# Encoder trunk with three token mixers: both passes over a block traced with a scheduling priority of 4000

## The chip, the cores and the metric

The kernel runs on one core of one Trainium2 chip. The metric is the device time of one execution in microseconds (us). TensorE (PE) does the matmuls, VectorE (DVE) and ScalarE (ACT) the element-wise work, GpSimd (POOL) a little of it, and SyncE (SP) issues most of the transfers.

## The reference, cut to what matters

Two sequences (256 and 2048 rows of 1024) go through one encoder layer. Each layer has a projection whose columns feed three mixers, each of which scans the sequence forward and backward in chunks; then an output projection, a gated feed-forward block and norms.

```python
h = _rmsnorm(x, prm['norm_mix'][l])
p = h @ prm['w_in'][l]
pg, pr, ps = _split(p, [GLA_COLS, RWKV_COLS, SSD_COLS])
o_gla  = _gla_mixer(pg, ...)     # forward scan + strict backward scan
o_rwkv = _rwkv7_mixer(pr, ...)   # the same, with a 64x64 state per head
o_ssd  = _ssd_mixer(ps, ...)     # the same, after a convolution over 5 rows
mix = jnp.concatenate([o_gla, o_rwkv, o_ssd], axis=-1)
x = x + mix @ prm['w_out'][l]
h = _rmsnorm(x, prm['norm_ffn'][l])
x = x + (jax.nn.silu(h @ prm['ffn_gate'][l]) * (h @ prm['ffn_up'][l])) @ prm['ffn_down'][l]
return _rmsnorm(x, prm['final_norm'])
```

## The kernel before, in words

The 2304 rows are cut into nine blocks of 256 (block 0 is the prompt, 1 to 8 the sample) and, for the wide matmuls, into groups of up to 512 rows (the sample's begin at rows 256, 768, 1280 and 1792).

There are two kinds of work. **Panels** are the wide matmuls: `in_chan` and `in_tok` (input projection), `out_proj`, and the steps of `ffn`. A panel loads 256 columns of a weight (`wr`), splits them into a high and a low part (`wh` on ACT, `wl` on DVE), and runs three matmuls for each 128 rows of the contraction, in fp32r, with the full 128x128 array, into PSUM tiles `d` and `g`. The normed and transposed input of a group sits in the tile pair `hT`, of which there is one: the next group's four transposes and copies (`norm_T`, L371) wait until the last panel of a group has read it.

**Passes** are the mixers. `pass_a(b)` does the forward scans of block b and stores what the backward scan needs; `pass_b(b)` does the backward scans and leaves the result in the tile pair `mix`, which `out_proj(b)` reads. A pass is a long chain of small fp32 matmuls (PSUM tiles `s`, `c`, `a` and, in `pass_a`, `g`) with DVE and ACT instructions between them. Many of these matmuls use a part of the array: `prod` (in `rwkv_local`) multiplies 32x32 pieces, 32 matmuls to a product, into two `s` tiles, `rwkv_chain` works on 64x64 pieces into `c`.

All instructions are traced once, in the order in which the Python runs; a scheduler then orders them on each engine: of the instructions that are ready it takes the one with the lowest number first, which is its place in the trace. `high_priority(offset=n)` traces a stretch with n taken off that number. Before the change this is used for norms alone (offset 3000, in `normed` and in `ffn`). `run` sets the trace order: panels of a group, then `pass_a` of the blocks that are complete, then the next group; later `second(...)` yields after each `pass_b`, and two steps of `ffn` follow each yield. `first` and `second` are the two closures that call the passes.

Every matmul goes through `mm`, so the profile gives all of them line 118; they are told apart by their tiles.

Of the kernel before, what the change touches and what calls it, by code (L numbers as in the profile page):

```python
# [70 lines left out]
class Encoder:  # L71
# [1066 lines left out]
    def run(self):  # L1138
        self.setup()
        prompt = [(t, min(GS, self.Lp - t)) for t in range(0, self.Lp, GS)]  # L1140
        sample = [(t, min(GS, self.NT - t)) for t in range(self.Lp, self.NT, GS)]
        done, st, sb, self.rs2, self.ready = 0, None, None, {}, {}

        def first(end):

            nonlocal done, st
            while done < self.NB:
                lo, hi = self.seq(done)
                need = (done + 1) * TB
                if need > end or (need == end and need != hi):  # L1150
                    break
                if done * TB == lo:
                    st = self.states()
                self.pass_a(done, st)
                done += 1

        def second(t0, n):

            nonlocal sb
            mix = None  # L1160
            for b in range((t0 + n) // TB - 1, t0 // TB - 1, -1):
                if (b + 1) * TB == self.seq(b)[1]:
                    sb = self.states()
                if mix is not None:
                    self.out_proj(b + 1, mix)
                mix = self.pass_b(b, sb)
                self.free = False
                yield
            self.out_proj(t0 // TB, mix)

        def run(*steps):

            steps = list(steps)
            while steps:
                for s, k in list(steps):
                    for _ in range(k):
                        if next(s, steps) is steps:
                            steps.remove((s, k))
                            break

        def emit(steps, k=None):
            while (k is None or k > 0) and next(steps, steps) is not steps:
                k = k and k - 1

        order = sample[::-1]
        self.last = order[0][0]
        for t0, n in prompt:
            emit(self.in_proj(t0, n))
            if t0 == 0:
                self.setup_mixers()  # L1190
            first(t0 + n)
        ahead = [second(*g) for g in reversed(prompt)]
        for k, (t0, n) in enumerate(sample):
            dense = self.in_proj(t0, n, 2 if k or len(sample) == 1 else 0)
            if k == 1 or k == len(sample) - 1:
                for s in ahead:
                    emit(s, 1)
                    emit(dense, 5)
                    emit(s)
                ahead = []  # L1200
                first(t0)
            if k > 0 or len(sample) == 1:
                emit(dense, 11)
                first(t0 + n)
            emit(dense)
        if len(sample) > 1:
            emit(self.in_proj(*sample[0], 1))
        early = [self.ffn(*g, inside=g[1] <= TB) for g in prompt]
        for f in early:
            emit(f, 2)  # L1210
        rest = [self.ffn(*g, after) for g, after in zip(order, order[1:] + [None])]
        for k, f in enumerate(early + rest):
            steps = [(second(*order[k]), 1)] if k < len(order) else []
            run(*steps, (f, 2))
# [30 lines left out]
```

## Time and profile before

| | |
|---|---|
| median of 3 runs | 3809.86 us (3805.5 to 3811.69) |
| the profiled execution | 3807.3 us, span 3805.4 us |
| PE busy | 3574.5 us, 94% |
| DVE busy | 2417.1 us, 64% |
| ACT busy | 1464.8 us, 38% |
| POOL busy | 589.9 us, 16% |
| mean granted TensorE clock | 0.963 of 2.4 GHz |

The span is the time between the first and the last instruction; the profiled execution's own time is 1.9 us more. Matmuls are pipelined, so PE's busy time is an upper bound of its work. The granted clock of a stretch is a mean over two levels, 1.2 and 2.4 GHz: 0.77 means that the clock was at 1.2 GHz for 46% of that stretch.

### The profile page before, as it was taken

The numbers are of one execution on the slowest core, as the hardware profiler recorded it, in microseconds if no ns is written. First come the engines' busy times: TensorE is split into PE (matmuls) and PEld (weight loads), VectorE is DVE, ScalarE is ACT, GpSimd is POOL, SyncE is SP. The second block draws the span as 40 slices with busy tenths as digits, with TensorE's granted clock in tenths as the row PEclk, the third lists the DMA queues.
The fourth block names the chain that finished last, engine by engine and source line by source line (L and its number), as shares of the span: only waits on it lengthen the run. The fifth ranks groups of instructions, "written<-read, shape, count | busy, mean of one in ns | idle before, by whom it ended". The sixth has DMA issues, their size and how long they took to land.

```text
span 3805.4 us, 84415 instructions
## 1 busy us (share of the span) xinstructions
PE 3574.5 (94%) x34142; PEld 3002.8 (79%) x34142; DVE 2417.1 (64%) x5533; ACT 1464.8 (38%) x3282; POOL 589.9 (16%) x618
## 2 busy tenths in 40 slices
PE   6899889899989989998989999999999999999998
PEld 6677667677767767887978888888888888888887
DVE  5943496785883798876757564665655565545444
ACT  4623253543553455443433232323233232332222
POOL 3422123242332333211000000000000000000000
PEclk9999899899989989998989999999999999999999
DMA  6544243334334433554644343434343442434332
GB/s 180 169 143 126 84 144 114 118 106 134 120 97 126 128 115 121 167 170 142 192 134 136 113 140 116 141 114 131 117 139 115 131 137 86 148 100 139 94 95 95
DMA packets 430230, 486.87 MB, mean 128 GB/s; under 512 B 49344, under 2 KB 389584, under 8 KB 428688
## 3 DMA queue, kind: packets, MB, share of 16 engines
q1 hardware_dynamic: 390720, 422.40, 36.4%
q10 hardware_dynamic: 38112, 55.40, 4.1%
q8 instruction: 269, 4.41, 0.5%
q0 software_dynamic: 1008, 3.67, 0.3%
q14 instruction: 121, 0.99, 0.1%
HBM read 395.18 MB, written 86.18 MB: 126 GB/s over the span
## 4 chain that ended last, share of the span: by engine, by line
PE 73%; DVE 15%; DMA 6%; ACT 3%; issue 3%; POOL 0%; ACTq 0%; SPq 0%; DVEq 0%; POOLq 0%
PE d L118 46%; PE g L118 15%; PE s L118 4%; PE a L118 3%; PE c L118 3%; DVE mix L104 3%; DVE wl L94 1%; DMA mix<-d_xb 1%; DMA x<-d_x 1%; DVE mix L94 1%; PE d L371 1%; DVE b4a L94 1%; DMA qg<-q_g 1%; DVE b9x L104 1%; ACT wh L111 1%
## 5 line engine op out<-in xcount | busy, mean ns | idle before, releaser
L118 PE MATMUL d<-hT,wh 128*128 128x512 f32 (+3 forms) x4384 | 1276.7, 376 | 19.3 <-DVE ev L115 10.0
L111 ACT ACTIVATE wh<-wr 128x512 fp32r<-128x512 f32 (+1 forms) x1084 | 624.8, 621 | 1146.0 <-PE d L118 638.0
L94 DVE TENSOR_TENSOR wl<-wr,wh 128x512 fp32r<-128x512 f32 x944 | 650.8, 717 | 475.2 <-ACT wh L111 471.2
L118 PEld LDWEIGHTS d<-hT,wh 128*128 128x128 f32 (+1 forms) x4384 | 791.2, 191 | 174.1 <-issue 13.3
L118 PE MATMUL d<-hT,wl 128*128 128x512 f32 (+3 forms) x2192 | 813.0, 374 | 8.5 <-DVE wl L94 8.4
L118 PEld LDWEIGHTS d<-hT,wl 128*128 128x128 f32 (+1 forms) x2192 | 417.2, 191 | 85.9 <-DVE wl L94 11.4
L94 POOL TENSOR_TENSOR wl<-wr,wh 128x512 fp32r<-128x512 f32 (+1 forms) x140 | 202.0, 1444 | 583.7 <-ACT wh L111 519.5
L118 PE MATMUL g<-hT,wh 128*128 128x512 f32 x896 | 282.3, 394 | 0.0
L118 PE MATMUL d<-wh,b 128*128 128x256 f32 x928 | 267.3, 289 | 3.3 <-DVE b4d L94 2.4
L118 PE MATMUL d<-wl,b 128*128 128x256 f32 x928 | 259.9, 281 | 0.0
L118 PE MATMUL d<-wh,b9x 128*128 128x256 f32 x928 | 258.6, 282 | 0.0
L118 PE MATMUL d<-wh,hT 128*128 128x256 f32 x1216 | 251.1, 298 | 3.2 <-DVE ev L115 2.4
L118 PEld LDWEIGHTS d<-wh,hT 128*128 128x128 f32 x1216 | 200.5, 197 | 14.6 <-issue 4.7
L118 PEld LDWEIGHTS g<-hT,wh 128*128 128x128 f32 x896 | 166.3, 188 | 34.4 <-issue 0.3
L118 PE MATMUL d<-wh,mix 128*128 128x256 f32 x832 | 173.6, 295 | 10.1 <-ACT mix L111 7.5
L118 PEld LDWEIGHTS d<-wh,b 128*128 128x128 f32 x928 | 174.8, 188 | 10.0 <-DVE b4d L94 3.0
L118 PE MATMUL d<-wl,hT 128*128 128x256 f32 x608 | 177.4, 294 | 3.6 <-DVE wl L94 3.6
L118 PEld LDWEIGHTS d<-wl,b 128*128 128x128 f32 x928 | 174.9, 189 | 0.9
L118 PE MATMUL g<-hT,wl 128*128 128x512 f32 x448 | 175.1, 391 | 0.0
L118 PEld LDWEIGHTS d<-wh,b9x 128*128 128x128 f32 x928 | 174.2, 189 | 0.7 <-issue 0.3
L118 PEld LDWEIGHTS d<-wh,mix 128*128 128x128 f32 x832 | 138.1, 196 | 13.7 <-ACT mix L111 8.4
L118 PE MATMUL g<-wh,b 128*128 128x256 f32 x480 | 140.0, 292 | 2.3 <-DVE b4a L94 2.0
(387 smaller groups left out, 6149.7 us busy)
## 6 DMA issues: line engine op xcount, KB each, us to landing
wr<-in_w_in SPq DMA_DIRECT2D x260, 256.0 KB, 3.1
wr<-in_ffn_gate SPq DMA_DIRECT2D x220, 256.0 KB, 2.8
wr<-in_ffn_up SPq DMA_DIRECT2D x220, 256.0 KB, 2.9
wr<-in_ffn_down SPq DMA_DIRECT2D x220, 256.0 KB, 2.9
wr<-in_w_out SPq DMA_DIRECT2D x144, 256.0 KB, 3.1
x<-in_x_sample SPq DMA_DIRECT2D x20, 512.0 KB, 3.9
x<-d_x SPq DMA_DIRECT2D x20, 512.0 KB, 3.8
q_s<-qs ACTq DMA_DIRECT2D x18, 520.0 KB, 3.4
```

What stands on the lines that cost most here:

```text
L94: (eng or self.nc.vector).tensor_tensor(out=out, in0=a, in1=b, op=op)
L104: (eng or self.nc.vector).scalar_tensor_tensor(out=out, in0=a, scalar=s, in1=b, op0=op0, op1=op1)
L111: self.nc.scalar.activation(out=out, in_=in_, func=AF.Copy)
L118: self.nc.tensor.matmul(out, lhsT=lhsT, rhs=rhs, start=start, stop=stop, tile_position=tp, skip_group_check=lax)
L371: self.nc.tensor.transpose(ps[:, k * P:(k + 1) * P], h[:, (4 * q + k) * P:(4 * q + k + 1) * P], self.c["ident"])
```

## The change

Each pass is traced in a `high_priority(offset=4000)` block. No instruction is added, removed or altered; their order on the engines changes.

```diff
@@ -1151,7 +1151,8 @@
                     break
                 if done * TB == lo:
                     st = self.states()
-                self.pass_a(done, st)
+                with self.tc.high_priority(offset=4000):
+                    self.pass_a(done, st)
                 done += 1
 
         def second(t0, n):
@@ -1163,7 +1164,8 @@
                     sb = self.states()
                 if mix is not None:
                     self.out_proj(b + 1, mix)
-                mix = self.pass_b(b, sb)
+                with self.tc.high_priority(offset=4000):
+                    mix = self.pass_b(b, sb)
                 self.free = False
                 yield
             self.out_proj(t0 // TB, mix)
```

**First place, PE at the end of `pass_b` of block 0.** `s_4062`, `s_4068`, `a_4130` and `a_4167` belong to that pass, `c_5684`, `s_5182`, `s_5183`, `s_5196`, `s_5197` to `pass_a` of block 1, and `d_4812` is the first panel of `out_proj` of block 0, which reads the pass's result. PE's rows before the change:

```order
L118 MATMUL s_4062<-qy_3511,cf 128x256 x2
L118 MATMUL c_5684<-b9x_5157,gup 128x256 x2
L118 MATMUL s_4068<-cf,b2a_4066 128x2 x4
L118 MATMUL s_5182<-b9x_5157,wup 64x256 x4
L118 MATMUL s_5183<-b9x_5157,wup 64x256 x4
L118 MATMUL s_4068<-ident,b2a_4066 128x128 x4
L118 MATMUL s_5196<-b9x_5157,aup 64x256 x4
L118 MATMUL a_4130<-cf,b2a_4128 128x2 x4
L118 MATMUL a_4167<-sS_3500,scb_4160 128x256 x2
L118 MATMUL s_5197<-b9x_5157,aup 64x256 x4
L118 MATMUL a_4130<-ident,b2a_4128 128x128 x4
L118 MATMUL d_4812<-wh,mix_199_3502 128x256
```

After the change (`d_4423` is the first panel of the group of row 768):

```order
L118 MATMUL d_4423<-hT_4240,wh 128x512
L118 MATMUL d_4423<-hT_4241,wh 128x512
L118 MATMUL d_4423<-hT_4240,wl 128x512
L118 MATMUL a_4130<-cf,b2a_4128 128x2 x4
L118 MATMUL a_4167<-sS_3500,scb_4160 128x256 x2
L118 MATMUL s_5197<-b9x_5157,aup 64x256 x4
L118 MATMUL d_4423<-hT_4240,wh 128x512
L118 MATMUL d_4423<-hT_4241,wh 128x512
L118 MATMUL d_4423<-hT_4240,wl 128x512
```

Before, the five panels of that group stand ahead of the end of the pass, and between `s_4062` and `d_4812` no panel matmul stands. After it the end of the pass has moved ahead of most of them: between `s_4062` and the last matmul into `a_4130` stand 83 panel matmuls of 512 columns.

**Second place, PE in the first product of `pass_b` of block 4**, written to `s_28130` and `s_28131`; the rows into `g` and `d` are panels (before: of `out_proj` of block 5). Before:

```order
L118 MATMUL g_26491<-wl,mix_1921_24512 128x256
L118 MATMUL g_26491<-wh,mix_1922_24513 128x256
L118 MATMUL s_28130<-BK_28051,qg_28061 32x32 x3
L118 MATMUL s_28131<-BK_28051,qg_28061 32x32
L118 MATMUL d_26490<-wh,mix_1921_24512 128x256
L118 MATMUL g_26491<-wh,mix_1921_24512 128x256
L118 MATMUL s_28131<-BK_28051,qg_28061 32x32 x3
L118 MATMUL s_28130<-BK_28051,qg_28061 32x32
L118 MATMUL d_26490<-wl,mix_1921_24512 128x256
L118 MATMUL d_26490<-wh,mix_1922_24513 128x256
```

After, with panels of `ffn` around it:

```order
L118 MATMUL d_25644<-wh,b_2010_25250 128x256
L118 MATMUL d_25644<-wl,b_2010_25250 128x256
L118 MATMUL s_28130<-BK_28051,qg_28061 32x32 x4
L118 MATMUL s_28131<-BK_28051,qg_28061 32x32 x4
L118 MATMUL s_28130<-BK_28051,qg_28061 32x32 x4
L118 MATMUL s_28131<-BK_28051,qg_28061 32x32 x4
L118 MATMUL s_28130<-BK_28051,qg_28061 32x32 x4
L118 MATMUL s_28131<-BK_28051,qg_28061 32x32 x4
L118 MATMUL s_28130<-BK_28051,qg_28061 32x32 x4
L118 MATMUL s_28131<-BK_28051,qg_28061 32x32 x4
L118 MATMUL d_25644<-wh,b9x_25251 128x256
```

The same 32 matmuls stand in nine pieces before, strewn among panels, and in one piece after.

## Rows read from the trace of the kernel before

**Rows 1.** The page: span, busy time of each engine, chain by engine.

```profile
span 3805.4 us, 84415 instructions
...
PE 3574.5 (94%) x34142; PEld 3002.8 (79%) x34142; DVE 2417.1 (64%) x5533; ACT 1464.8 (38%) x3282; POOL 589.9 (16%) x618
...
PE 73%; DVE 15%; DMA 6%; ACT 3%; issue 3%; POOL 0%; ACTq 0%; SPq 0%; DVEq 0%; POOLq 0%
```

**Rows 2.** Busy time by stretch: stretch, length, engines (records), PEclk, DMA share, GB/s.

```profile
428.00:511.00 83.00, 64.00 (x518) 53.42 (x518) 64.04 (x166) 30.59 (x70) 11.95 (x13) 0.77 0.37 114
...
688.00:750.00 62.00, 47.57 (x845) 32.16 (x837) 54.45 (x126) 41.51 (x116) 22.43 (x26) 0.88 0.36 108
...
1049.00:1102.00 53.00, 41.42 (x422) 30.75 (x421) 52.28 (x133) 31.25 (x81) 16.00 (x19) 0.77 0.32 96
...
1367.00:1412.00 45.00, 33.29 (x318) 23.63 (x319) 41.30 (x101) 27.42 (x69) 17.08 (x18) 0.81 0.33 102
...
1719.00:1751.00 32.00, 23.66 (x240) 19.48 (x238) 18.08 (x56) 4.52 (x10) 4.68 (x6) 0.68 0.30 97
1751.00:1905.00 154.00, 150.77 (x1894) 140.06 (x1895) 116.35 (x308) 69.71 (x171) 11.77 (x14) 0.99 0.59 184
1905.00:1940.00 35.00, 25.17 (x531) 20.75 (x532) 21.41 (x63) 11.62 (x31) 0.79 (x2) 0.71 0.56 184
1940.00:3255.00 1315.00, 1298.91 (x11391) 1114.36 (x11391) 788.03 (x1860) 423.85 (x908) 76.34 (x85) 1.00 0.39 123
3255.00:3805.00 550.00, 531.02 (x3124) 470.09 (x3123) 271.10 (x574) 170.23 (x343) 1.14 (x2) 0.99 0.35 112
```

**Rows 3.** Timeline of PE, 428 to 475: rows with idle before them.

```profile
431.71 1.98 PE L118 MATMUL s<-qy,cf 128*128 128x256 f32 x4 [0.72 <-DVE qy L94]
...
453.61 2.08 PE L118 MATMUL a<-ident,b2a 128*128 128x128 f32 x8 [3.54 <-DVE b2a L104]
461.13 0.58 PE L118 MATMUL d<-wh,mix 128*128 128x256 f32 x1 [5.45 <-ACT mix L111]
469.26 0.99 PE L1054 MATMUL a<-ident,b2b 128*128 128x128 f32 x4 [2.87 <-DVE b2b L104]
```

**Rows 4.** Timeline of PE in a torn product, 2262.7 to 2265.3: start, us.

```profile
2262.73 0.28 PE L118 MATMUL g<-wh,mix 128*128 128x256 f32 x1
2262.85 0.28 PE L118 MATMUL g<-wl,mix 128*128 128x256 f32 x1
...
2264.02 0.28 PE L118 MATMUL g<-wh,mix 128*128 128x256 f32 x1
2264.23 0.26 PE L118 MATMUL s<-BK,qg 32*32 32x32 f32 x8
2264.43 0.38 PE L118 MATMUL d<-wh,mix 128*128 128x256 f32 x1
2264.65 0.28 PE L118 MATMUL g<-wh,mix 128*128 128x256 f32 x1
2264.86 0.26 PE L118 MATMUL s<-BK,qg 32*32 32x32 f32 x8
2265.05 0.39 PE L118 MATMUL d<-wl,mix 128*128 128x256 f32 x1
```

**Rows 5.** Timeline of PE where a product stands in one piece.

```profile
1004.76 0.76 PE L118 MATMUL s<-W,BK 32*32 32x32 f32 x64
1005.44 0.69 PE L118 MATMUL c<-UV,SC 128*64 128x64 f32 x16
```

**Rows 6.** Timeline of PE: an fp32 transpose on the full array between panel matmuls.

```profile
2198.70 0.39 PE L118 MATMUL d<-hT,wl 128*128 128x512 f32 x1
2198.93 0.39 PE L118 MATMUL d<-hT,wh 128*128 128x512 f32 x1
2199.16 1.05 PE L118 MATMUL s<-ident,b2a 128*128 128x128 f32 x8
```

**Rows 7.** The costliest groups: a panel's matmuls that read `wl`.

```profile
L118 PE MATMUL d<-hT,wl 128*128 128x512 f32 (+3 forms) x2192 | 813.0, 374 | 8.5 <-DVE wl L94 8.4
```

## The prediction

> **What bounds the kernel now.** I read the page first: PE is busy 94% of the span, and the chain that ended last is PE for 73% and DVE for 15% [rows 1]. So the end is set by PE's work and by the places where PE waits. The busy times by stretch say where those are. From 1940 to 3255 us, where `ffn` panels run beside `pass_b` of blocks 5 to 1, PE is busy 1298.9 of 1315 us at full clock; from 3255 on there are panels alone [rows 2]. There only less PE work helps. Before 1940 there are short stretches in which PE waits: 19.0 us of 83 are idle from 428 to 511, and in the three stretches in which `hT` is filled anew for the next group (from 688, 1049 and 1367) PE is busy 122.3 of 160 us while DVE is busy 148.0 of 160. In all four the granted clock is 0.77 to 0.88 [rows 2]: after the idling PE works part of the time at 1.2 GHz, so an idle microsecond there costs more than itself. The timeline says what the first stretch is: the end of `pass_b` of block 0, a chain with nothing beside it. PE waits 3.54 us for DVE's `b2a`, then 5.45 us before the first matmul of `out_proj`, for `mix` [rows 3]. From the matmul into `s` at 431.71 to the one into `a` at 453.61 that is 22 us without a panel.
>
> **What the change moves.** Panels and passes compete for PE, DVE, ACT and the queues. Before, a panel traced ahead of a pass goes first whenever it is ready, and the pass gets what is left over; now a pass goes first and the panels fill. The work is the same, so only the order can pay, and I looked in the two built orders for what changes at the places above. Durations are from the trace, counts from the orders.
>
> *The end of block 0's pass.* It now stands ahead of most of the group of row 768: 83 panel matmuls of 512 columns lie between the pass's `s_4062` and the last one into `a_4130`, where before there was none. Such matmuls follow each other after 0.23 us [rows 6], so that is 19 us of cover for a chain that took 22. What the stretch loses now: 19.0 us idle, and the clock. At 0.77 it ran at 1.2 GHz for 46% of 83 us, 38 us; if all of the idle time lay within those, 19 us of work took twice its time (9.5 us lost), and if none did, 38 (19 lost). So 28.5 to 38 us are lost, of which I take **25** as won, since 19 of 22 us are covered and `pass_a` of block 1 has waits of its own there. Bounds: nothing (the waits turn up again under that pass) and 38.
>
> *Torn products.* In the stretch from 1940 to 3255 the products of `rwkv_local` come in pieces, since panels went first: the first one of block 4's pass stands in nine pieces among panels, and after the change in one. What a piece costs is in the timeline. Panel matmuls of 256 columns start 0.12 us apart; where the next one is a 32x32 matmul it starts 0.21 us later, so 0.09 more. The four matmuls (eight records) then hold PE for 0.20 us before the panel goes on [rows 4]; as a part of a whole product, 64 records in 0.68 us [rows 5], eight take 0.085. So there is another 0.115, and a piece pays 0.2 us, **0.10 for each change** of the part of the array in use. It isn't fp32 that costs: an fp32 transpose on the full 128x128 starts 0.23 us after a panel matmul, as the next panel matmul does [rows 6]. So I counted in both orders where neighbouring matmuls use a different part of the array. Among the matmuls that ran from 1940 to 3255: 552 before, 328 after. From 1612 to 1940: 204 and 161. Before 1612: 720 and 696. In the first two stretches 267 fewer by 0.10 is **26.7 us**; the 24 earlier ones I put at nothing, since PE waits for DVE in much of that part. In the long stretch PE idles 16 of 1315 us, so little there can swallow the gain. Bounds: nothing, and 291 by 0.10, 29.
>
> The Trainium skill has two rules for this. "TensorE: Matmul & The Clock Gate" (Step-by-step: what each phase is for) says that the drain of one matmul overlaps the fill of the next, so that a stream is spaced by its columns alone; by that a torn product costs nothing, and the sum would lack this term. "TensorEngine Tiling (Array Packing)" (Key Properties) says that a change of the tiling mode, not of the tile alone, drains TensorE. The rows side with the second: 0.21 against 0.12 us where the part changes, no difference where it doesn't.
>
> *The refilling of `hT`.* Norms have offset 3000, passes now 4000, so a norm's DVE steps give way to a pass. But the passes have less left to do there: between the first and the last DVE write of `hT` stood 73, 71 and 50 pass instructions in the three stretches, and now 46, 60 and 49. At 148.0 us for the 360 DVE instructions of the three [rows 2], 0.41 us each, the 39 that went are 16 us of DVE. They run elsewhere, so I count **nothing**, between a gain of 16 and the loss of the first rival.
>
> *Cover in between, DVE, queues.* Panels that now stand beside passes are missing elsewhere. I gave each matmul of the orders its usual spacing (0.227 us for 512 columns, 0.119 for 256, 0.014 for 32x32, and so on) and cut the part from `pass_a` of block 1 to that of block 8 into slices of 20 us: panels have under 40% in 11 of 46 slices before, in 8 of 48 after. So the cover is as even as it was: nothing. A panel's `wl` is made on DVE and now gives way to passes; of all the panel matmuls that read `wl` into `d` those waits are 8.4 us [rows 7], and DVE is busy 788 of 1315 us in the long stretch [rows 2]: nothing. Loads of a pass stand earlier in SP's queue, ahead of weight loads; they are still placed behind the stores that they read, and I count nothing for them. From 3255 on the orders are alike.
>
> **Sum.** 3807.3 (the profiled execution) - 25 - 26.7 = 3755.6. The median of the runs is 2.6 us over the profiled execution: **3758 us**, 1.4% less.
>
> **Rivals.**
>
> *The norms starve (slower).* A pass that is ready always goes before the norm on DVE, which is already busy 148 of 160 us there. The 194 pass instructions of the three stretches are 80 us of DVE; if the norms wait for about that much more, panels start that much later, and the time is 3758 + 80 = 3838. It decides from 52 us on, 17 for each refill. Against it: 155 instructions are left there, not more. 0.12.
>
> *It cancels.* The waits of the first place turn up again where `pass_a` runs with few panels, and the bunching costs what the whole products save: 3758 + 52 = 3810. For it: four of the stretches that lose time have DVE at 77 to 99%, and a pass that is sooner ready is sooner there as well. "Perfetto Trace Analysis" (Optimization Strategy) advises to interleave stretches with different bounds, and passes first is rather the opposite; the slices above don't show it. 0.10.
>
> *Only the first place pays.* PE's extra 0.2 us for a piece is a wait in disguise that a whole product has too: 3758 + 27 = 3785. This is what the first of the two rules gives. Against it: the rows show no wait at these matmuls. 0.10.
>
> *The later ends of passes are cured as well.* From 1719 to 1751 and from 1905 to 1940 PE idles 8.3 and 9.8 us, and runs at 0.68 and 0.71 of the clock [rows 2]: 64% and 58% of these stretches, 20 us each, at 1.2 GHz, of which about half is idle, so some 10 us more are lost: 28 in all, and 3730. For it: passes finish sooner. Against it: both orders have a run of pass matmuls alone ahead of `out_proj` of block 8. 0.13.
>
> **How the numbers follow.** My forecast has 0.55, with 3738 to 3783 for itself: 20 us less where the first place gives 38 and the refills something, 25 more where the first place gives nothing. A measurement of this kernel tells 0.2% (7.6 us) from no change. Faster is the forecast, the third and the fourth rival, 0.78, and a little of the second: 0.79. The same is most of the second, 0.09; slower is the first, 0.12. The range leaves out the first rival and part of the second: 3724 (the fourth with 6 us of the earlier changes and refills) to 3802.
>
> **What would show it.** Right: in the new trace the first matmul of `out_proj` of block 0 comes right behind panel matmuls, and PE idles under 5 us in the 80 us around the end of that pass, at a clock over 0.95. Products of `pass_b` in the `ffn` part stand as single rows of 64 records, and the time from the first `ffn` step of row 1792 to the last `out_proj` shrinks by some 22 us with PE still at 98% or more. The three refills keep about 160 us in sum. The prediction is wrong if the refills grow by 17 us each, if PE's idle time before 1612 stays and only changes place, or if the `ffn` part keeps its length.

## The result and the profile after

The changed kernel takes **3747.97 us** (median of 5 runs, 3743.01 to 3754.97), the kernel before 3808.57 on the same chip (5 runs): ratio 0.9844, 95% interval 0.9826 to 0.9863. That is 60.6 us less; forecast were 3758 us and a range of 3724 to 3802.

The page of the changed kernel, its span, busy times and chain by engine:

```profile
span 3747.8 us, 84453 instructions
...
PE 3519.5 (94%) x34142; PEld 2981.5 (80%) x34142; DVE 2413.4 (64%) x5533; ACT 1462.5 (39%) x3282; POOL 592.0 (16%) x618
...
PE 69%; DVE 16%; DMA 8%; ACT 3%; issue 3%; SPq 0%; POOL 0%; ACTq 0%; DVEq 0%; POOLq 0%
```

Beside [rows 1] the span is 57.6 us shorter and PE's busy time 55.1 us, with the same number of matmuls. PE's idle time is nearly what it was: 230.9 us before, 228.3 after. So the same matmuls take less time: fewer of them run at the low clock (by the clock rows of the two traces PE is busy at 1.2 GHz for 224 us before and 191 after; at twice the speed the 33 between them are worth 16), and fewer change the part of the array in use. On the whole there is no less waiting.

The busy times by stretch of the changed kernel, columns as in [rows 2]:

```profile
428.00:511.00 83.00, 78.36 (x1104) 63.67 (x1103) 71.86 (x188) 48.49 (x127) 18.61 (x21) 1.00 0.58 181
596.00:672.00 76.00, 63.49 (x917) 51.03 (x915) 51.67 (x111) 36.32 (x86) 20.24 (x21) 0.89 0.38 118
728.00:771.00 43.00, 34.12 (x542) 25.97 (x541) 42.09 (x101) 27.37 (x77) 18.24 (x22) 0.80 0.37 115
1029.00:1090.00 61.00, 43.50 (x617) 30.75 (x615) 50.12 (x123) 32.79 (x88) 24.87 (x27) 0.78 0.34 111
1347.00:1393.00 46.00, 35.00 (x353) 26.77 (x353) 40.58 (x98) 27.02 (x65) 14.62 (x18) 0.70 0.44 142
1900.00:3190.00 1290.00, 1270.06 (x11209) 1102.50 (x11208) 775.58 (x1844) 422.53 (x902) 71.92 (x81) 0.99 0.40 124
```

From 428 to 511, where PE idled 19.0 of 83 us at a clock of 0.77 [rows 2], it idles 4.6 at 1.00. Row two is a new poor stretch: 12.5 of 76 us idle, clock 0.89. The three refills of `hT` (rows three to five; the first of them runs on to 774) take 150 us in sum, 160 before, and PE idles 37 us in them, 38 before.

What stands around the first matmul of `out_proj` of block 0, in the timeline of PE of the changed kernel:

```profile
449.73 0.39 PE L118 MATMUL a<-s,k 128*128 128x32 f32 x2
449.96 0.37 PE L118 MATMUL d<-wh,mix 128*128 128x256 f32 x1
450.16 0.28 PE L118 MATMUL d<-wl,mix 128*128 128x256 f32 x1
...
472.17 0.36 PE L118 MATMUL d<-wh,mix 128*128 128x256 f32 x1 [2.25 <-DVE xo L94]
```

The 5.45 us for `mix` and the 3.54 us for `b2a` [rows 3] are gone; the longest wait of this stretch is now 2.25 us.

The small matmuls themselves, in the groups that keep shapes apart. The two costliest 32x32 groups before:

```profile
L118 PE MATMUL s<-W,BK 32*32 32x32 f32 x3744 | 60.5, 202 | 7.9 <-ACT BK L111 7.7
L118 PE MATMUL s<-BK,qg 32*32 32x32 f32 x2016 | 35.6, 203 | 9.7 <-DVE BK L634 7.9 <-DVE so L94 1.7
```

and the same two after:

```profile
L118 PE MATMUL s<-W,BK 32*32 32x32 f32 x3744 | 47.1, 200 | 0.6 <-ACT BK L111 0.3 <-issue 0.3
L118 PE MATMUL s<-BK,qg 32*32 32x32 f32 x2016 | 24.9, 197 | 1.3 <-ACT BKt L111 1.3
```

The number is the same and the mean duration nearly so, but the busy time, in which overlapping records count once, falls by 13.4 and 10.7 us: the records of a whole product overlap each other more. In the `ffn` part they now stand in whole rows (timeline of the changed kernel):

```profile
2000.54 0.75 PE L118 MATMUL s<-W,BK 32*32 32x32 f32 x64
...
2006.44 0.75 PE L118 MATMUL s<-BK,qg 32*32 32x32 f32 x64
```

### The profile page after: what moved, and what is told of

The parts are those of the page before. It is cut to its first block, busy times and chain, and to the rows that moved or that the text cites. A ratio compares the mean times of both kernels' runs of the same rounds, so it can differ in the third digit from the quotient of the medians.

```text
span 3747.8 us, 84453 instructions
## 1 busy us (share of the span) xinstructions
PE 3519.5 (94%) x34142; PEld 2981.5 (80%) x34142; DVE 2413.4 (64%) x5533; ACT 1462.5 (39%) x3282; POOL 592.0 (16%) x618
## 4 chain that ended last, share of the span: by engine, by line
PE 69%; DVE 16%; DMA 8%; ACT 3%; issue 3%; SPq 0%; POOL 0%; ACTq 0%; DVEq 0%; POOLq 0%
PE d L118 43%; PE g L118 14%; PE s L118 4%; PE a L118 3%; DVE mix L104 3%; PE c L118 3%; DVE wl L94 2%; DMA mix<-d_xb 1%; DMA wr<-in_w_out 1%; DVE mix L94 1%; DMA x<-d_x 1%; DMA b<-d_rk 1%; DVE b4a L94 1%; PE d L371 1%; DVE rx L104 1%
## 5 line engine op out<-in xcount | busy, mean ns | idle before, releaser
L118 PE MATMUL d<-hT,wh 128*128 128x512 f32 (+3 forms) x4384 | 1258.7, 372 | 11.5 <-ACT ev L111 6.6
L118 PEld LDWEIGHTS d<-hT,wh 128*128 128x128 f32 (+1 forms) x4384 | 782.2, 189 | 163.7 <-issue 11.1
L94 POOL TENSOR_TENSOR wl<-wr,wh 128x512 fp32r<-128x512 f32 (+1 forms) x140 | 211.1, 1509 | 508.9 <-ACT wh L111 400.2
L118 PE MATMUL d<-wh,hT 128*128 128x256 f32 x1216 | 263.6, 308 | 18.9 <-DVE hr L101 10.3
L118 PEld LDWEIGHTS d<-wh,hT 128*128 128x128 f32 x1216 | 210.5, 206 | 30.9 <-ACT wh L111 10.7
L118 PEld LDWEIGHTS d<-wh,b 128*128 128x128 f32 x928 | 175.5, 189 | 12.5 <-DVE b4d L94 5.7
L118 PE MATMUL d<-wh,mix 128*128 128x256 f32 x832 | 163.3, 285 | 7.1 <-ACT wh L111 3.8
L104 DVE SCALAR_TENSOR_TENSOR mix<-mix,cwh,mix 128x256 f32<-128x256 f32 x288 | 142.7, 543 | 26.5 <-ACT mix L107 26.3
```

The lines of the kernel that those rows point to most:

```text
L94: (eng or self.nc.vector).tensor_tensor(out=out, in0=a, in1=b, op=op)
L104: (eng or self.nc.vector).scalar_tensor_tensor(out=out, in0=a, scalar=s, in1=b, op0=op0, op1=op1)
L118: self.nc.tensor.matmul(out, lhsT=lhsT, rhs=rhs, start=start, stop=stop, tile_position=tp, skip_group_check=lax)
```

## Where the time went, at equal work

The orders differ, so times can't be compared at the same microsecond. I gave each matmul of an order its usual spacing, as in the prediction, and read from each trace when so many microseconds of this work had begun. The table gives the difference to the kernel before (minus is sooner) and in brackets that in changes of the array's part up to there. The kernels e1 to e11 are told of below. PE's order in e2 is that of the kernel before up to some 1000, and its times there still differ by up to 4 us: so much a single trace scatters.

| work, us | time before | change | e1 | e2 | e3 | e4 | e6 | e8 | e11 |
|---|---|---|---|---|---|---|---|---|---|
| 300 | 404.6 | 5 (-20) | 0 (-6) | 4 (0) | 2 (-26) | 0 (-10) | 2 (-6) | -5 (-15) | -2 (-6) |
| 400 | 562.9 | -36 (-28) | -41 (-15) | 3 (0) | 11 (-17) | -23 (-21) | -39 (-15) | -46 (-24) | -43 (-15) |
| 500 | 683.7 | -19 (-8) | -42 (-12) | 2 (0) | 15 (-1) | -24 (-17) | -38 (-12) | -47 (-19) | -42 (-10) |
| 1000 | 1333.5 | -34 (-37) | -63 (-13) | -1 (0) | 4 (-28) | -23 (-6) | -64 (-13) | -59 (-22) | -48 (-2) |
| 1400 | 1866.8 | -36 (-48) | -54 (-2) | 1 (-17) | -2 (-27) | -18 (-10) | -59 (-22) | -53 (-27) | -40 (-20) |
| 2700 | 3312.4 | -56 (-291) | -54 (-11) | -19 (-260) | 9 (-36) | -31 (-122) | -70 (-265) | -89 (-277) | -75 (-271) |

The change gains 41 us between 300 and 400, loses 17 from 400 to 500, has them back by 1000, and gains 20 from 1400 to 2700, while 243 changes of part go. From there on nothing changes.

## The experiments

All are the kernel before with the edit shown, unless it says otherwise. A first pass is `pass_a`, a second pass `pass_b`. Times are medians, beside the kernel before measured along with them (3805.57 us for e1 to e4, 3807.18 for e5 to e8, 3806.23 for e9 to e11); the span of numbers in brackets behind a ratio is its 95% interval.

**e1_block0: the second pass of block 0 alone.**

```diff
-                mix = self.pass_b(b, sb)
+                with (self.tc.high_priority(offset=4000) if b == 0 else ExitStack()):
+                    mix = self.pass_b(b, sb)
```

> Priority 4000 for pass_b of block 0 alone; every other pass as before. In its order the end of that pass again stands beside panels of the group of row 768, and changes of the array's part number 1465 (before 1476, after 1185). Theory (the first place and the whole products are two separate gains): 35 us under the kernel before, all of it between 400 and 500 us, nothing in the ffn part. Rival (the wait only moves, and pass_a must be ahead as well for it to stay away): under 10 us. Rival (it is the passes' long chain from block 1 to 8 that got shorter): under 10 us too.

Measured: 3754.29 us, ratio 0.9860 (0.9847 to 0.9873), 51 us less. The first place alone, by stretch, before, in the change and in e1, over the same work (300 to 400):

```profile
405.00:563.00 158.00, 128.82 (x1163) 100.51 (x1164) 117.71 (x303) 68.37 (x157) 32.14 (x33) 0.84 0.39 119
```
```profile
410.00:527.00 117.00, 111.04 (x1304) 88.04 (x1305) 102.80 (x264) 64.69 (x160) 30.06 (x30) 1.00 0.55 169
```
```profile
405.00:522.00 117.00, 112.04 (x1048) 91.47 (x1047) 96.71 (x237) 62.46 (x148) 24.02 (x26) 0.97 0.56 167
```

158 us become 117 in both. Before, 29.2 us were idle and, at 0.84, some 51 us ran at 1.2 GHz; in the change 6.0 are idle at full clock. So 23 of the 41 us are idle time and 18 busy time, nearly all of it the clock: PE was busy for 38 of the 51 us at 1.2 GHz, which is worth 19. The pass of block 0 is responsible by itself. In e1 it gains another 22 us from 400 to 1000, where the granted clock is low for 55 us instead of 89 and PE idles 7 us less, and gives back some 9 later.

**e2_b_1to8: the second passes of blocks 1 to 8 alone.**

```diff
-                mix = self.pass_b(b, sb)
+                with (self.tc.high_priority(offset=4000) if b > 0 else ExitStack()):
+                    mix = self.pass_b(b, sb)
```

> Priority 4000 for pass_b of blocks 1 to 8 alone. Its order is that of the kernel before up to pass_a of block 7, and from the second half of pass_b on that of the changed kernel: changes of the array's part 1216, 260 fewer than before. Theory: 260 by 0.10 is 26 us under the kernel before, all of it after 1612 us. Rival (a piece costs nothing that a whole product doesn't cost too): under 8 us. Rival (passes ahead help the dense part because its mixers are finished early): the gain comes in one place, not in proportion to the changes saved.

Measured: 3788.48 us, ratio 0.9952 (0.9939 to 0.9964), 17 us less. The table puts all of it in the `ffn` part: 20 us from 1400 to 2700, with 243 fewer changes. So the gain of the whole products is real, but some 0.08 us for each change, not 0.10. Where the rest is, the same stretch of work shows, 1400 to 2700, before and in the change:

```profile
1867.00:3312.00 1445.00, 1418.20 (x12665) 1220.09 (x12665) 875.25 (x2090) 478.16 (x1039) 77.12 (x87) 0.99 0.41 128
```
```profile
1831.00:3257.00 1426.00, 1391.69 (x12636) 1213.29 (x12633) 861.29 (x2070) 477.85 (x1038) 76.15 (x87) 0.99 0.42 130
```

PE's busy time falls by 26.5 us, 0.11 for each of 243 changes, as forecast; but its idle time rises from 26.8 to 34.3 us. The longest of the new waits in this stretch of the changed kernel (who waited for whom: us, times, longest):

```profile
PE c L118 <- DVE W L115: 6.2, 2, 5.7
PE d L118 <- ACT wh L111: 4.8, 7, 1.5
PE d L118 <- DVE b4d L94: 3.9, 2, 2.3
```

Before, `b4d` stood at 1.2 us in this stretch, and the other two were not among the longest waits:

```profile
PE d L118 <- DVE b4d L94: 1.2, 2, 0.6
```

`wh` and `b4d` are what panels need next from ACT and DVE, which a pass that goes first now has ahead of them; that this is the reason is argued from the names, not shown.

**e3_a_only: the first passes alone.**

```diff
-                self.pass_a(done, st)
+                with self.tc.high_priority(offset=4000):
+                    self.pass_a(done, st)
```

> Priority 4000 for pass_a alone. The end of pass_b of block 0 stands ahead of out_proj of block 0 as before, and products of pass_b are torn as before (1440 changes of part, 36 fewer). Theory: 0 to 8 us under the kernel before, since pass_a ahead only moves cover about. Rival (the chain of pass_a from block 1 to 8 is what bounds the part to 1612 us): 25 us or more under it.

Measured: 3813.28 us, ratio 1.0017 (1.0007 to 1.0026): 8 us more. The first place is not cured (timeline of PE of e3):

```profile
459.93 2.08 PE L118 MATMUL a<-ident,b2a 128*128 128x128 f32 x8 [5.38 <-DVE b2a L104]
465.17 0.58 PE L118 MATMUL d<-wh,mix 128*128 128x256 f32 x1 [3.16 <-ACT mix L111]
```

So this half of the change is a small loss. The three parts together (51 + 17 - 8 = 60 us) are what the change gains, 60.6.

**e4_prod: only the matmuls of the torn products.** `prod` is the function in `rwkv_local` that issues them.

```diff
-            for j in range(4):
-                for i in range(2):
-                    for g, o in to:
...
+            with self.tc.high_priority(offset=4000):
+                for j in range(4):
+                    for i in range(2):
+                        for g, o in to:
...
```

> The kernel before with priority 4000 for the matmuls of prod alone (the 32 small ones of each product), not for the passes. Changes of part 1354, 122 fewer than before, of which 101 in the ffn part; the end of pass_b of block 0 as before. Theory (0.10 us a change): 12 us under the kernel before, 10 of them after 1940 us. Rival (not the tearing costs but that passes come late): 0.

Measured: 3774.81 us, ratio 0.9911 (0.9896 to 0.9927), 31 us less. The sum was off since I had expected the end of the second pass of block 0 as before, and nothing from it. In the trace that end has moved: 103 panel matmuls of 512 columns start between `s_4062` and the last one into `a_4130`, where before there was none, and the first matmul of `out_proj` starts at 436.5 us, not 461.1. This place gains 23 us. In the `ffn` part e4 gains 13 us with 112 fewer changes, 0.12 each.

**e7_price: a change of part by itself.** A program that leaves the whole computation out and writes zeros: two dense matmuls and one small product in turn, 96 times, and then the same matmuls in 12 whole groups.

```python
for small in (p32, p64, full):
    for _ in range(96):
        dense(2)      # 128x256, full array
        small(1)      # 4 matmuls of 32x32 or 64x64, or one fp32 128x128
    dense(100)
    for _ in range(12):
        dense(16)
        small(8)
    dense(100)
```

> A program by itself, which leaves the whole computation out and writes zeros. It alternates two dense 128x256 matmuls with one small product of 4 matmuls 96 times (torn), and then runs the same matmuls in 12 groups of 16 dense ones and 8 products (whole); this for small matmuls of 32x32, for 64x64, and for one fp32 product on the full 128x128 array. Torn has 168 more changes of the array's part than whole. Theory A (a change costs about 0.10 us, as the gaps around torn products show): torn minus whole is about 17 us for 32x32 and for 64x64, and about 0 for the full array. Rival (the gaps around torn products were waits for other engines or the issue of the weights, not the change of part): about 0 for the small ones, or as much for the full array as for them.

Measured, in the timeline of PE (each fp32 matmul is two records): torn and then whole, for 32x32,

```profile
58.06 0.50 PE L101 MATMUL d<-hi,lo 128*128 128x256 f32 x2
58.49 0.26 PE L106 MATMUL s<-x 32*32 32x32 f32 x8
58.68 0.50 PE L101 MATMUL d<-hi,lo 128*128 128x256 f32 x2
...
103.47 2.17 PE L101 MATMUL d<-hi,lo 128*128 128x256 f32 x16
105.58 0.75 PE L106 MATMUL s<-x 32*32 32x32 f32 x64
106.26 1.46 PE L101 MATMUL d<-hi,lo 128*128 128x256 f32 x10
```

and for the fp32 product on the full array:

```profile
299.65 0.48 PE L101 MATMUL d<-hi,lo 128*128 128x256 f32 x2
299.96 0.39 PE L115 MATMUL f<-x 128*128 128x128 f32 x2
300.11 0.48 PE L101 MATMUL d<-hi,lo 128*128 128x256 f32 x2
...
360.91 2.16 PE L101 MATMUL d<-hi,lo 128*128 128x256 f32 x16
362.90 1.95 PE L115 MATMUL f<-x 128*128 128x128 f32 x16
364.61 2.16 PE L101 MATMUL d<-hi,lo 128*128 128x256 f32 x16
```

Torn, a turn with 32x32 takes 0.625 us (start to start, a mean over the stretch); whole, 2.79 us for eight, 0.349 each. The 0.276 between them pays for 1.75 changes: 0.158 us each, 26.5 us for the 168. With 64x64 the turns take 0.810 and 0.515 us, 0.169 for each change:

```profile
170.85 0.45 PE L111 MATMUL s<-x 64*64 64x64 f32 x8
171.66 0.45 PE L111 MATMUL s<-x 64*64 64x64 f32 x8
...
240.00 2.18 PE L101 MATMUL d<-hi,lo 128*128 128x256 f32 x16
244.12 2.18 PE L101 MATMUL d<-hi,lo 128*128 128x256 f32 x16
```

On the full array they take 0.46 both times, nothing. So it is the change of part that costs, not the smallness of the product nor fp32, and where nothing else is in the way it costs more than I read from [rows 4]. The Trainium skill's rule that the drain of one matmul overlaps the fill of the next ("TensorE: Matmul & The Clock Gate", Step-by-step: what each phase is for), from which the third rival took that tearing costs nothing, fits e7 on the full array only. The Trainium skill's rule that a change of tiling mode drains TensorE ("TensorEngine Tiling (Array Packing)", Key Properties) agrees with the 0.158 and 0.169 us; that it is a drain which takes this time, no run here shows.

**e5_norm5000: the change, with the norms ahead of both passes again.**

```diff
-        with self.tc.high_priority(offset=3000):
+        with self.tc.high_priority(offset=5000):
```

(the same at the norms in `ffn`.)

> The change, with the norms' own offset raised from 3000 to 5000, so that they stand ahead of both passes as they do in the kernel before. Theory A (the norms do not starve, since the three refills take 150 us in sum after the change and 160 before): within 4 us of the change, 3744 to 3752. Rival (the passes take VectorE from the norms, and what the change gains is net of it): faster than the change by 10 us or more, with the three refills below 140 us in sum.

Measured: 3743.75 us, ratio 0.9831 (0.9814 to 0.9849), not to be told from the change. The refills do get shorter: from the start of the first to that of the last DVE write of `hT` the three take 143 us before, 132 in the change and 93 here (in a run that was 10 us faster than the median). For 39 us less of refill the median moves by 4 us. Each ratio is known to some 7 us either way, so the 10 us that the rival asked for are not seen, but not ruled out; the norms hold the change back by little, if at all.

**e6_b_all: the second passes of all blocks, the first passes as before.**

```diff
-                with self.tc.high_priority(offset=4000):
-                    self.pass_a(done, st)
+                self.pass_a(done, st)
```

(against the change.)

> The second pass of every block is traced 4000 ahead; the first pass keeps its place, as in the kernel before. Theory A (the parts add up: block 0's second pass gives 51 us, those of blocks 1 to 8 give 17, and the first pass ahead costs 7): 3806 - 51 - 17 = 3738 us, 7 to 10 us below the change, with the cost of the change in the 80 us behind 596 us (the loads of gv and gl, which the matmuls wait for) gone. Theory B (moving both passes together is what keeps the two in step, so the first pass alone costs but beside the second it doesn't): 3745 to 3750, as the change. A second pass that runs ahead of everything while the first one waits for what it leaves: 3755 or more.

Measured: 3737.69 us, ratio 0.9813 (0.9795 to 0.9831): as theory A had it, and 10 us below the change. The two intervals (the change has 0.9826 to 0.9863) only just touch.

**e9_no_gla and e10_gla_only: which half of the first pass costs.** Both on e6. In e9 the first pass up to `rwkv_chain` and the steps of `ssd_a` are ahead, `gla_a` isn't; in e10 only `gla_a` is.

```diff
         for n in "sgggss":
-            next(both[n], None)
+            with self.tc.high_priority(offset=4000 if n == "s" else 0):
+                next(both[n], None)
```

(this for e9, where the lines ahead of it also stand in a block of 4000; in e10 they keep their place, and `"s"` is `"g"`.) What suggested it is the longest wait of PE from 410 to 665 in the changed kernel, the new poor stretch, which e6 lacks there:

```profile
PE g L118 <- DMA gv<-d_v: 5.1, 1, 5.1
```

> Both passes ahead as in the change, but of the first pass the part of the gated linear attention (which loads gv and gl from DRAM behind the stores of in_proj) keeps its own place. Theory A (what the first pass ahead costs are matmuls of that part, placed early, that wait for their loads: 5.1 us for gv in one place): as with the second passes alone, 3738 us, at most 3742. Rival (it is the rest of the first pass, which takes DVE and PE from panels that would go first): 3745 to 3750, as the change. The order has 80 more changes of the array's part before 1612 us than with the second passes alone; at 0.10 to 0.16 us each, if none is hidden by waits, 8 to 13 us more.

> The second passes ahead, and of the first pass only the part of the gated linear attention. Theory A (its early matmuls wait for their loads): 3744 to 3750, as much as the change. Rival (the rest of the first pass costs): 3738, as with the second passes alone.

Measured: 3756.59 us, ratio 0.9864 (0.9845 to 0.9884), and 3754.39, ratio 0.9858 (0.9840 to 0.9876). Both are slower than e6 by 17 to 19 us, and neither is faster than the change, which has both halves ahead. Neither half is harmless, so theory A falls, and so does its rival. In e9 no load is among the longest waits, but up to 1400 the order has 81 more changes of part than e6 (at 0.12 us some 10 of the 19), and the waits are spread over many short ones. The profiled runs lie 13 us under the median in e9 and 11 over it in e10, so a comparison of their traces tells little. What the first pass's place costs is, in e9 at least, not a load.

**e8_b_all_prod and e11_prod_b: the products ahead of the rest of the pass.** Both on e6, with the edit of e4; in the second passes the two offsets add up, so `prod` stands 4000 ahead of its own pass. In e11 the offset is `4000 * d`, nothing in a first pass (`d` is 0 there).

> As the kernel with all second passes ahead, and of the first pass only the matmuls of prod are ahead too. If whole products are worth 0.10 us for each change of the array's part that they save, the order saves 12 more changes, about 1 us: the same time as that kernel within 3 us. If what the first pass ahead costs comes from its products displacing other matmuls, and not from its loads and gates, then 5 to 8 us slower than that kernel.

> The second passes ahead, and inside them the matmuls of prod another 4000 ahead; the first pass's prod keeps its place (in the kernel with all prod ahead it was moved too, and that was 18 us faster than with the second passes alone). By the profile of that kernel 7 us of the 18 stand before 400 us, where passes of both kinds run, and 11 after 1612 us, where only second passes are left. Theory A (the two parts are what they seem): 3738 - 11 = 3727 us or, if the early 7 us are the second pass of block 0, 3720. Rival (it is the first pass's products in both places): 3738.

Measured: e8 **3719.60 us**, ratio 0.9765 (0.9748 to 0.9782), the best version, 28 us below the change and 18 below e6, where I had expected nothing; e11 3728.68, ratio 0.9796 (0.9781 to 0.9811), 9 us below e6, whose interval it overlaps. From 1400 to 2700 in e6 and in e8:

```profile
1808.00:3243.00 1435.00, 1397.00 (x12638) 1217.65 (x12639) 863.62 (x2071) 478.18 (x1038) 75.36 (x87) 0.98 0.41 130
```
```profile
1814.00:3224.00 1410.00, 1382.06 (x12634) 1205.94 (x12629) 869.29 (x2070) 478.64 (x1038) 76.32 (x87) 0.99 0.42 132
```

Against e6, PE idles 27.9 us instead of 38.0 and is busy 15 us less, with only 7 changes fewer; the granted clock is low for 20 us of this stretch instead of 51. PE's waits for `wh` into `d` fall from 8.2 to 3.0 us, those for `W` from 7.1 to 5.1, those for `b4d` from 4.3 to 1.3. So this part of the gain is in waits and the clock: idle time that came with the whole products is taken back. (The change, with 34.3 us idle and 37 at the low clock, lies between.)

e11 gains as much here (35 us in the table, e8 36, e6 11), more than the 11 us over e6 that its theory A had; but from 500 to 1000 it falls 20 us behind e6, which no theory had and no run explains. That its median comes out at theory A's 3727 is luck.

## Why the prediction was right

**The end of block 0's pass** was the right place by the right mechanism, and too small: forecast 25 us, measured 41 (change and e1). The step that was off is the window. I priced 83 us from 428 to 511, with 19.0 us idle and 38 at 1.2 GHz, 28 of them busy: 33 us lost. The same weakness reaches from 405 to 563, with 29.2 idle and 51 at the low clock, 38 of them busy: 48 lost, of which 41 were won. My lower bound, "nothing", is refuted at this place.

But the second rival, by which the waits turn up again under `pass_a`, is not refuted for the part behind it, and one of my own signs of being wrong nearly came: that PE's idle time before 1612 us stays and only changes place. Up to the work that had begun by 1612 us, in the kernel before, the change and e6:

```profile
0.00:1612.00 1612.00, 1440.80 (x15442) 1141.33 (x15446) 1121.07 (x2488) 739.00 (x1717) 482.97 (x496) 0.93 0.42 128
```
```profile
0.00:1591.00 1591.00, 1424.02 (x15535) 1136.25 (x15536) 1131.01 (x2495) 735.45 (x1717) 490.51 (x501) 0.94 0.43 131
```
```profile
0.00:1564.00 1564.00, 1418.45 (x15530) 1125.26 (x15531) 1129.18 (x2496) 739.12 (x1717) 475.04 (x501) 0.96 0.44 133
```

PE idles 171 us before, 167 in the change and 146 in e6 (142 in e1). So in the change most of the 23 us of idle time won at the first place has come back by then, and 21 us of time are left; e1 and e6, whose first passes keep their place, keep it.

**Torn products**: forecast 26.7 us from 1612 on. From 1400 to 2700 the busy time falls by 26.5 us with 243 fewer changes, and 7.5 us return as waits (3 of them in the stretch that I had called long), 19 net; e2 by itself gives 17 us in all. Cut at 1612 us, as in the forecast, the change gains 21 us before and 36 behind; but e2, with the same second passes, has 20 behind, so the rest of the 36 isn't the products. The step that was off is that nothing would swallow the gain, on the grounds that PE idled so little there and that DVE had room: the term was too large by about 7 us, the waits. The price of 0.10 was a little low. If PE's busy time at 1.2 GHz is counted half, its busy time in this stretch falls by 0.12 to 0.13 us for each change saved in the change, e2, e6, e8 and e11 (in e4 by 0.08). What is left of it after waits and clock goes from 0.05 (e6, 11 us for 243) to 0.14 (e8, 36 for 250). e7 shows that the change of part has a price of its own, 0.16 to 0.17 us where nothing hides it.

**First passes ahead** I had counted at nothing under the cover in between. They cost 8 us alone (e3) and 10 beside the second passes (the change against e6). A place where they do can be seen in the profile (596 to 672 us: 12.5 us idle, clock 0.89, with 5.1 us on the load of `gv`), but e9 and e10 don't single out a cause; that stays open.

**Refills and norms**: forecast 160 us in sum, measured 150. The first rival, 17 us more for each refill, is refuted by that.

**The other rivals.** "Only the first place pays" is refuted by e2 and e7. "It cancels" is refuted for the sum by the time of the change. "Later ends of passes are cured as well" didn't come: from work 1000 to 1900, which holds both places, PE idles about 55 us before and 60 after.

So the sum hides errors of opposite sign: +16 at the first place, -7 at the products, and a cost of the first passes, which part of block 0's further gain covers. That forecast and measurement (52 and 61 us) lie so near is in part luck. That the parts add up (e1, e2, e3 to 60 where the change has 60.6; e1 and e2 to 68 where e6 has 69) is shown for these three parts only; e9 and e10 show that it doesn't hold for every cut.

## What to carry to other kernels

When a stretch has idle time and a low granted clock, price it over all of its length, to where the clock is back at full: here 18 of 41 us were clock, and a window that was too narrow left out 15 of the 48 us that were lost. Where small tiled matmuls are mixed with full ones, count the changes of the array's part in the order: keeping a product in one piece pays 0.05 to 0.14 us for each here, by what waits and clock leave of it, and it can be done for the matmuls of that product alone. Put ahead what something else waits for at the end of a chain (the second passes and the products in them), and test what stands beside it (the first passes) by itself, since it may cost.

## What was not expected of the hardware

A change of the array's part costs 0.158 us to and from 32x32 matmuls and 0.169 to and from 64x64 ones in a dense stream, and nothing for fp32 matmuls on the full array (e7). In the `ffn` part e6 and e8 differ by 7 changes and by 25 us: 10 of them are idle time, and most of the rest goes with the granted clock, low for 51 us in e6 and 20 in e8.
